# Layer normalisation without affine terms: hand-placed semaphores, tiles of 8 rows and a VectorE loop in place of a scheduled, unrolled kernel

## Chip, cores, metric

One core of a Trainium2 chip. The metric is the device time of one execution in microseconds, the median of several runs; smaller is better. The granted TensorE clock was 1.0 (TensorE does nothing in this kernel). Before: 318.19 us (318.15 to 318.25, 3 runs).

## The reference

```python
x: float32 [32, 512, 1024]            # 16384 rows of 1024; eps = 1e-5
mean = np.mean(x, axis=-1, keepdims=True)
var  = np.var(x, axis=-1, keepdims=True)
out  = (x - mean) / np.sqrt(var + eps)
```

The core has 128 partitions, so 16384 rows are 128 "rows per partition". Below, "a tile of 8 rows" means 8 rows in each of the 128 partitions, 4.2 MB.

## The kernel before

A ring of 50 rows per partition in SBUF holds the tiles. SyncE issues the loads, VectorE (DVE in the profile) takes the statistics of each half row (`bn_stats`), GpSimd (POOL) joins them in nine small steps, ScalarE (ACT) takes the root, VectorE the reciprocal, and ScalarE normalises in place and issues the store. Semaphores are placed by the scheduler. A load must wait until the store that last used its rows has landed.

```python
TILES = (4, 6, 10, 10, 10, 10, 10, 10, 10, 10, 10, 10, 10, 6, 2)
RING = 50
GROUP = 10        # rows normalised together
FINE = 6          # ... in the last LAST tiles
LAST = 3
...
    def rows_of(a, row, K):          # partition p gets K rows that lie together in memory
        return a[row * P : (row + K) * P].rearrange("(p k) d -> p k d", p=P)

    def group(xs, G):
        for k in range(G):
            for s in range(NSUB):    # two halves of 512
                nc.vector.bn_stats(out=stats[:, k, s, :], in_=xs[:, k, s * BN_MAX : (s + 1) * BN_MAX])
        ...                          # nine GpSimd steps, from stats to nmean and ss
        nc.scalar.activation(out=std[:, :G], in_=ss[:, :G], func=AF.Sqrt, bias=eps_t, scale=1.0 / D)
        nc.vector.reciprocal(out=rstd[:, :G], in_=std[:, :G])
        nc.gpsimd.tensor_mul(out=nmr[:, :G], in0=nmean[:, :G], in1=rstd[:, :G])
        for k in range(G):
            nc.scalar.activation(out=xs[:, k, :], in_=xs[:, k, :], func=AF.Identity,
                                 bias=nmr[:, k : k + 1], scale=rstd[:, k : k + 1])
    ...
    with tc.manual_schedule():
        nc.vector.memset(eps_t, eps_val)
        for t, (K, row, pos) in enumerate(plan):
            nc.sync.dma_start(out=ring[:, pos : pos + K, :], in_=rows_of(x2, row, K))
            step = FINE if t >= len(TILES) - LAST else GROUP
            for g in range(0, K, step):
                group(ring[:, pos + g : pos + g + min(step, K - g), :], min(step, K - g))
            nc.scalar.dma_start(out=rows_of(o2, row, K), in_=ring[:, pos : pos + K, :])
```

Of the kernel before, what the change touches and what calls it, by code (L numbers as in the profile page):

```python
# [1 line left out]

# [4 lines left out]


TILES = (4, 6, 10, 10, 10, 10, 10, 10, 10, 10, 10, 10, 10, 6, 2)  # L10

RING = 50


GROUP = 10
FINE = 6
LAST = 3


@with_exitstack  # L20
def kernel(
    ctx: ExitStack,
    tc: tile.TileContext,
    x: bass.AP,
    eps: bass.AP,
    out: bass.AP,
):
    nc = tc.nc
    P = nc.NUM_PARTITIONS
    eps_val = float(eps) if not isinstance(eps, bass.AP) else 1e-5  # L30

    x2 = x.flatten_outer_dims()
    o2 = out.flatten_outer_dims()
    N, D = x2.shape
    BN_MAX = nc.vector.BN_STATS_FMAX
    NSUB = D // BN_MAX
    H = 2 * NSUB
    assert sum(TILES) * P == N

    rings = ctx.enter_context(tc.tile_pool(name="rings", bufs=1))  # L40
    st = ctx.enter_context(tc.tile_pool(name="st", bufs=3))
    sm = ctx.enter_context(tc.tile_pool(name="sm", bufs=10))

    fdt = mybir.dt.float32
    AF = mybir.ActivationFunctionType
    ALU = mybir.AluOpType

    ring = rings.tile([P, RING, D], fdt)
    eps_t = rings.tile([P, 1], fdt)

    def rows_of(a, row, K):
        return a[row * P : (row + K) * P].rearrange("(p k) d -> p k d", p=P)

    def pool_sum(o, terms):
        G = terms.shape[1]
        half = sm.tile([P, GROUP, 2], fdt, name="half")
        nc.gpsimd.tensor_tensor(  # L57
            out=half[:, :G], in0=terms[:, :, 0:2], in1=terms[:, :, 2:4], op=ALU.add
        )
        nc.gpsimd.tensor_tensor(  # L60
            out=o, in0=half[:, :G, 0], in1=half[:, :G, 1], op=ALU.add
        )

    def group(xs, G):
        stats = st.tile([P, GROUP, NSUB, 6], fdt, name="stats")
        for k in range(G):
            for s in range(NSUB):
                nc.vector.bn_stats(  # L68
                    out=stats[:, k, s, :],
                    in_=xs[:, k, s * BN_MAX : (s + 1) * BN_MAX],  # L70
                )

        parts = stats[:, :G].rearrange("p g s (h c) -> p g (s h) c", h=2)
        mean4, m2 = parts[:, :, :, 1], parts[:, :, :, 2]
        nmean = sm.tile([P, GROUP], fdt, name="nmean")
        dev = sm.tile([P, GROUP, H], fdt, name="dev")
        ss = sm.tile([P, GROUP], fdt, name="ss")
        pool_sum(nmean[:, :G], mean4)
        nc.gpsimd.tensor_scalar(  # L79
            out=nmean[:, :G], in0=nmean[:, :G], scalar1=-1.0 / H, scalar2=None, op0=ALU.mult  # L80
        )
        nc.gpsimd.tensor_tensor(  # L82
            out=dev[:, :G],
            in0=mean4,
            in1=nmean[:, :G].unsqueeze(2).to_broadcast([P, G, H]),
            op=ALU.add,
        )
        nc.gpsimd.tensor_mul(out=dev[:, :G], in0=dev[:, :G], in1=dev[:, :G])  # L88
        nc.gpsimd.tensor_scalar(  # L89
            out=dev[:, :G], in0=dev[:, :G], scalar1=float(D // H), scalar2=None, op0=ALU.mult  # L90
        )
        nc.gpsimd.tensor_tensor(out=dev[:, :G], in0=dev[:, :G], in1=m2, op=ALU.add)  # L92
        pool_sum(ss[:, :G], dev[:, :G])
        std = sm.tile([P, GROUP], fdt, name="std")
        nc.scalar.activation(  # L95
            out=std[:, :G], in_=ss[:, :G], func=AF.Sqrt, bias=eps_t, scale=1.0 / D
        )
        rstd = sm.tile([P, GROUP], fdt, name="rstd")
        nc.vector.reciprocal(out=rstd[:, :G], in_=std[:, :G])  # L99
        nmr = sm.tile([P, GROUP], fdt, name="nmr")  # L100
        nc.gpsimd.tensor_mul(out=nmr[:, :G], in0=nmean[:, :G], in1=rstd[:, :G])  # L101
        for k in range(G):
            nc.scalar.activation(  # L103
                out=xs[:, k, :],
                in_=xs[:, k, :],
                func=AF.Identity,
                bias=nmr[:, k : k + 1],
                scale=rstd[:, k : k + 1],
            )

    plan, row, pos = [], 0, 0
    for K in TILES:
        if pos + K > RING:
            pos = 0
        plan.append((K, row, pos))
        row += K
        pos += K

    with tc.manual_schedule():
        nc.vector.memset(eps_t, eps_val)  # L120
        for t, (K, row, pos) in enumerate(plan):
            nc.sync.dma_start(out=ring[:, pos : pos + K, :], in_=rows_of(x2, row, K))
            step = FINE if t >= len(TILES) - LAST else GROUP
            for g in range(0, K, step):
                G = min(step, K - g)
                group(ring[:, pos + g : pos + g + G, :], G)
            nc.scalar.dma_start(out=rows_of(o2, row, K), in_=ring[:, pos : pos + K, :])


# [1 line left out]
_INS = ['x', 'eps']  # L131
_OUTS = [((32, 512, 1024), 'float32')]

_NUMBERS = {'eps': 1e-05}


# [26 lines left out]
```

## Time and profile before

| What | Before |
|---|---|
| time, median | 318.19 us |
| span of the profiled execution | 316.6 us |
| VectorE, ScalarE, GpSimd busy | 49%, 48%, 12% |
| moved by DMA | 134.25 MB, 424 GB/s over the span |
| loads, stores: share of the 16 DMA engines | 49.6%, 49.1% |

Read it from the bottom up: the engines are half idle, and the last two rows say what they wait for. Two of before's lines give the first load and the first store; in this view of instructions in order of time, the columns are start, length, engine, line and operation:

```profile
0.72 8.16 SPq L122 DMA_DIRECT2D ring<-in_x_dram  x6
...
21.58 0.37 ACTq L127 DMA_DIRECT2D out_dram<-ring  x1
```

SyncE issues the first load at 0.72 us and six in a row; ScalarE issues the first store at 21.58 us. Between the two the DMA engines have only loads to do.

### The profile page before, as it was taken

Reading aid. Unit: us, or ns where it says so; the run is one execution under the profiler, and the core shown is the slowest. Engines: PE = TensorE matmul, PEld = TensorE weight load, DVE = VectorE, ACT = ScalarE, POOL = GpSimd, SP = SyncE. Lnnn points to the kernel's source line nnn. Section 1 sums busy time; section 2 is a strip of 40 time slices with the busy share of each in tenths; the row PEclk is TensorE's granted clock in tenths of the full one; section 3 lists DMA queues with packets and bytes.
Section 4 is the critical chain, followed back from the end, with each engine's and each line's share of the span. In section 5 each row is a group of like instructions: output and inputs, shape, how many; then the busy total and the mean of one; then the engine's idle time right before and its main releaser. Section 6 shows DMA issues by size and latency. Waiting matters only on the chain.

```text
span 316.6 us, 712 instructions
## 1 busy us (share of the span) xinstructions
DVE 156.5 (49%) x273; ACT 152.6 (48%) x145; POOL 37.5 (12%) x164
## 2 busy tenths in 40 slices
DVE  0692939539139229229319309409509509654300
ACT  1065329294490391291292192193094094591730
POOL 0202030200300300300300300300300200222200
DMA  8999999999999999999999999999999999999995
GB/s 308 437 424 401 411 466 430 432 419 440 446 435 414 430 457 430 424 419 466 430 424 419 450 435 436 414 430 445 450 414 424 450 438 408 444 421 426 463 407 247
DMA packets 4324, 134.25 MB, mean 424 GB/s; under 512 B 480, under 2 KB 480, under 8 KB 480
## 3 DMA queue, kind: packets, MB, share of 16 engines
q1 hardware_dynamic: 2160, 67.11, 49.6%
q10 hardware_dynamic: 2160, 67.11, 49.1%
q14 instruction: 4, 0.03, 0.0%
HBM read 67.11 MB, written 67.11 MB: 424 GB/s over the span
## 4 chain that ended last, share of the span: by engine, by line
DMA 42%; DVE 26%; another core or an unknown queue 14%; POOL 6%; ACT 5%; issue 3%; SPq 0%; DVEq 0%; POOLq 0%
DMA ring<-in_x_dram 29%; DVE stats L68 26%; DMA out_dram<-ring 13%; ACT ring L103 4%; POOL half L57 1%; POOL dev L89 1%; ACT std L95 1%; POOL dev L92 1%; POOL dev L82 1%; POOL nmean L79 1%; POOL dev L88 1%; POOL nmean L60 1%; POOL ss L60 1%; DVE rstd L99 0%
## 5 line engine op out<-in xcount | busy, mean ns | idle before, releaser
L68 DVE BATCH_NORM_STATS2 stats<-ring 128x6 f32<-128x512 f32 x256 | 153.4, 677 | 92.5 <-DMA ring<-in_x_dram 92.5
L103 ACT ACTIVATE ring<-ring,nmr,rstd 128x1024 f32<-128x1024 f32 x128 | 146.5, 1226 | 8.9 <-POOL nmr L101 8.9
L95 ACT ACTIVATE std<-ss,eps_t 128x10 f32<-128x10 f32 (+3 forms) x16 | 4.8, 301 | 141.7 <-POOL ss L60 141.7
L57 POOL TENSOR_TENSOR half<-stats 128x20 f32<-128x20 f32 (+3 forms) x16 | 3.7, 233 | 243.2 <-DVE stats L68 243.2
L99 DVE RECIPROCAL rstd<-std 128x10 f32<-128x10 f32 (+3 forms) x16 | 3.3, 204 | 51.7 <-ACT std L95 51.7
L89 POOL TENSOR_SCALAR dev<-dev 128x40 f32<-128x40 f32 (+3 forms) x16 | 4.6, 289 | 1.4
L101 POOL TENSOR_TENSOR nmr<-nmean,rstd 128x10 f32<-128x10 f32 (+3 forms) x16 | 3.3, 205 | 10.4 <-DVE rstd L99 10.4
L92 POOL TENSOR_TENSOR dev<-dev,stats 128x40 f32<-128x40 f32 (+3 forms) x16 | 4.1, 259 | 1.3
L79 POOL TENSOR_SCALAR nmean<-nmean 128x10 f32<-128x10 f32 (+3 forms) x16 | 3.9, 244 | 1.4
L82 POOL TENSOR_TENSOR dev<-stats,nmean 128x40 f32<-128x40 f32 (+3 forms) x16 | 3.9, 245 | 1.3
L88 POOL TENSOR_TENSOR dev<-dev 128x40 f32<-128x40 f32 (+3 forms) x16 | 3.8, 239 | 1.3
L57 POOL TENSOR_TENSOR half<-dev 128x20 f32<-128x20 f32 (+3 forms) x16 | 3.4, 212 | 1.3
L60 POOL TENSOR_TENSOR nmean<-half 128x10 f32<-128x10 f32 (+3 forms) x16 | 3.2, 203 | 1.3
L60 POOL TENSOR_TENSOR ss<-half 128x10 f32<-128x10 f32 (+3 forms) x16 | 3.2, 203 | 1.3
L95 ACT ACT_TABLE_LOAD x1 | 1.3, 1283 | 0.9 <-DVE eps_t L120 0.9
L120 DVE MEMSET eps_t<- 128x1 f32 x1 | 0.1, 59 | 0.8 <-PEq L144 0.8
L144 POOL MEMSET const-float32-0.0<- 128x1 f32 x1 | 0.1, 98 | 0.2 <-issue 0.2
L144 POOL MEMSET const-uint8-127<- 128x1 uint8 x1 | 0.1, 102 | 0.0
L144 POOL MEMSET const-bfloat16-1.0<- 128x1 bf16 x1 | 0.1, 101 | 0.0
L144 POOL MEMSET const-float32-1.0<- 128x1 f32 x1 | 0.1, 98 | 0.0
## 6 DMA issues: line engine op xcount, KB each, us to landing
ring<-in_x_dram SPq DMA_DIRECT2D x11, 5120.0 KB, 52.4
out_dram<-ring ACTq DMA_DIRECT2D x11, 5120.0 KB, 41.0
ring<-in_x_dram SPq DMA_DIRECT2D x2, 3072.0 KB, 30.7
out_dram<-ring ACTq DMA_DIRECT2D x2, 3072.0 KB, 22.0
ring<-in_x_dram SPq DMA_DIRECT2D x1, 2048.0 KB, 7.8
out_dram<-ring ACTq DMA_DIRECT2D x1, 2048.0 KB, 22.4
ring<-in_x_dram SPq DMA_DIRECT2D x1, 1024.0 KB, 61.0
out_dram<-ring ACTq DMA_DIRECT2D x1, 1024.0 KB, 11.4
```

Of the source, the lines that this page charges most:

```text
L57: nc.gpsimd.tensor_tensor(out=half[:, :G], in0=terms[:, :, 0:2], in1=terms[:, :, 2:4], op=ALU.add)
L60: nc.gpsimd.tensor_tensor(out=o, in0=half[:, :G, 0], in1=half[:, :G, 1], op=ALU.add)
L68: nc.vector.bn_stats(out=stats[:, k, s, :], in_=xs[:, k, s * BN_MAX : (s + 1) * BN_MAX],)
L79: nc.gpsimd.tensor_scalar(out=nmean[:, :G], in0=nmean[:, :G], scalar1=-1.0 / H, scalar2=None, op0=ALU.mult)
L82: nc.gpsimd.tensor_tensor(out=dev[:, :G], in0=mean4, in1=nmean[:, :G].unsqueeze(2).to_broadcast([P, G, H]), op=ALU.add,)
L88: nc.gpsimd.tensor_mul(out=dev[:, :G], in0=dev[:, :G], in1=dev[:, :G])
L89: nc.gpsimd.tensor_scalar(out=dev[:, :G], in0=dev[:, :G], scalar1=float(D // H), scalar2=None, op0=ALU.mult)
L92: nc.gpsimd.tensor_tensor(out=dev[:, :G], in0=dev[:, :G], in1=m2, op=ALU.add)
L95: nc.scalar.activation(out=std[:, :G], in_=ss[:, :G], func=AF.Sqrt, bias=eps_t, scale=1.0 / D)
L99: nc.vector.reciprocal(out=rstd[:, :G], in_=std[:, :G])
L101: nc.gpsimd.tensor_mul(out=nmr[:, :G], in0=nmean[:, :G], in1=rstd[:, :G])
L103: nc.scalar.activation(out=xs[:, k, :], in_=xs[:, k, :], func=AF.Identity, bias=nmr[:, k : k + 1], scale=rstd[:, k : k + 1],)
```

## The change

The intent: take the scheduler out of the way. One critical section with hand-placed semaphores replaces the scheduled block; all tiles but the last two have 8 rows and go round six fixed places; VectorE runs the middle twelve tiles as a loop of two turns, aligned so that its body sits in one block of instructions; the reciprocals are in that loop; all loads stay on SyncE's queue.

```diff
-TILES = (4, 6, 10, 10, 10, 10, 10, 10, 10, 10, 10, 10, 10, 6, 2)
-RING = 50
+TILES = (8,) * 15 + (6, 2)
+SLOT, SLOTS = 8, 6
+FIRST, TURNS = 3, 2
+BESIDE = ()                       # tiles whose load would go to ScalarE's queue
...
-    with tc.manual_schedule():
...
+    ctx.enter_context(tc.tile_critical(no_gpsimd_drain=True))
...
+    def vector(t, arrived, turn):
+        K, row, at = plan[t]
+        for k in range(K):
+            for s in range(NSUB):
+                i = nc.vector.bn_stats(...)
+                if k == 0 and s == 0:
+                    i._wait_ge(landed[t], arrived)
+        i.then_inc(taken, 1)
+        nc.vector.reciprocal(...)._wait_ge(rooted[t], turn).then_inc(inverse, 1)
...
+    for t in range(FIRST):
+        vector(t, 16, 1)
+    turn = nc.vector.alloc_register("turn")
+    nc.vector.reg_mov(turn, 1)
+    nc.vector.addr_align(128, max_nops=0)
+    with nc.vector.Fori(16, 16 * TURNS + 1, 16) as arrived:
+        for t in range(FIRST, FIRST + SLOTS):
+            vector(t, nc.vector.lower_val(arrived), turn)
+        nc.vector.reg_add(turn, turn, 1)
+    for t in range(FIRST + TURNS * SLOTS, len(plan)):
+        vector(t, 16, 1)
... (GpSimd's and ScalarE's steps: the same instructions, each with a hand-placed wait)
```

More of the change, by code (lines that the diff above doesn't have):

```diff
@@ L7 @@
 from concourse._compat import with_exitstack
-TILES = (4, 6, 10, 10, 10, 10, 10, 10, 10, 10, 10, 10, 10, 6, 2)
-RING = 50
-GROUP = 10
-FINE = 6
-LAST = 3
+TILES = (8,) * 15 + (6, 2)
+SLOT, SLOTS = 8, 6
+FIRST, TURNS = 3, 2
+BESIDE = ()
 @with_exitstack
@@ L38 @@
     assert sum(TILES) * P == N
-    rings = ctx.enter_context(tc.tile_pool(name="rings", bufs=1))
-    st = ctx.enter_context(tc.tile_pool(name="st", bufs=3))
-    sm = ctx.enter_context(tc.tile_pool(name="sm", bufs=10))
     fdt = mybir.dt.float32
@@ L46, with sbuf @@
     ALU = mybir.AluOpType
-    ring = rings.tile([P, RING, D], fdt)
-    eps_t = rings.tile([P, 1], fdt)
+    def sbuf(name, shape):
+        return ctx.enter_context(nc.sbuf_tensor(name, shape, fdt))
+    plan, row = [], 0
+    for K in TILES:
+        plan.append((K, row, row % (SLOT * SLOTS)))
+        row += K
+    ctx.enter_context(tc.tile_critical(no_gpsimd_drain=True))
+    ring = sbuf("ring", [P, SLOT * SLOTS, D])
+    stats = sbuf("stats", [P, SLOT * SLOTS, NSUB, 6])
+    half = sbuf("half", [P, SLOT, 2])
@@ new lines, with places @@
+    dev = sbuf("dev", [P, SLOT, H])
+    ss, nmean, std, rstd, nmr = (
+        sbuf(n, [P, SLOT * SLOTS]) for n in ("ss", "nmean", "std", "rstd", "nmr")
+    )
+    eps_t = sbuf("eps_t", [P, 1])
+    def places(name):
+        out = [nc.alloc_semaphore(f"{name}_{t}") for t in range(FIRST + SLOTS)]
+        for t in range(len(out), len(plan)):
+            looped = t < FIRST + TURNS * SLOTS
+            out.append(out[t - SLOTS] if looped else nc.alloc_semaphore(f"{name}_{t}"))
+        return out
@@ L51, in rows_of, with sixteens @@
+    def sixteens(sems, t):
+        return 16 * sum(1 for s in sems[: t + 1] if s.num == sems[t].num)
+    landed, rooted, stored = places("landed"), places("rooted"), places("stored")
+    taken, inverse, pool, act = map(
+        nc.alloc_semaphore, ("taken", "inverse", "pool", "act")
+    )
     def rows_of(a, row, K):
         return a[row * P : (row + K) * P].rearrange("(p k) d -> p k d", p=P)
-    def pool_sum(o, terms):
-        G = terms.shape[1]
-        half = sm.tile([P, GROUP, 2], fdt, name="half")
-        nc.gpsimd.tensor_tensor(
-            out=half[:, :G], in0=terms[:, :, 0:2], in1=terms[:, :, 2:4], op=ALU.add
-        )
-        nc.gpsimd.tensor_tensor(
-            out=o, in0=half[:, :G, 0], in1=half[:, :G, 1], op=ALU.add
-        )
@@ L64, in group @@
-    def group(xs, G):
-        stats = st.tile([P, GROUP, NSUB, 6], fdt, name="stats")
-        for k in range(G):
-            for s in range(NSUB):
-                nc.vector.bn_stats(
-                    out=stats[:, k, s, :],
-                    in_=xs[:, k, s * BN_MAX : (s + 1) * BN_MAX],
-                )
-        parts = stats[:, :G].rearrange("p g s (h c) -> p g (s h) c", h=2)
-        mean4, m2 = parts[:, :, :, 1], parts[:, :, :, 2]
-        nmean = sm.tile([P, GROUP], fdt, name="nmean")
-        dev = sm.tile([P, GROUP, H], fdt, name="dev")
-        ss = sm.tile([P, GROUP], fdt, name="ss")
-        pool_sum(nmean[:, :G], mean4)
-        nc.gpsimd.tensor_scalar(
-            out=nmean[:, :G], in0=nmean[:, :G], scalar1=-1.0 / H, scalar2=None, op0=ALU.mult
-        )
-        nc.gpsimd.tensor_tensor(
-            out=dev[:, :G],
-            in0=mean4,
-            in1=nmean[:, :G].unsqueeze(2).to_broadcast([P, G, H]),
-            op=ALU.add,
-        )
-        nc.gpsimd.tensor_mul(out=dev[:, :G], in0=dev[:, :G], in1=dev[:, :G])
-        nc.gpsimd.tensor_scalar(
-            out=dev[:, :G], in0=dev[:, :G], scalar1=float(D // H), scalar2=None, op0=ALU.mult
-        )
-        nc.gpsimd.tensor_tensor(out=dev[:, :G], in0=dev[:, :G], in1=m2, op=ALU.add)
-        pool_sum(ss[:, :G], dev[:, :G])
-        std = sm.tile([P, GROUP], fdt, name="std")
-        nc.scalar.activation(
-            out=std[:, :G], in_=ss[:, :G], func=AF.Sqrt, bias=eps_t, scale=1.0 / D
-        )
-        rstd = sm.tile([P, GROUP], fdt, name="rstd")
-        nc.vector.reciprocal(out=rstd[:, :G], in_=std[:, :G])
-        nmr = sm.tile([P, GROUP], fdt, name="nmr")
-        nc.gpsimd.tensor_mul(out=nmr[:, :G], in0=nmean[:, :G], in1=rstd[:, :G])
-        for k in range(G):
-            nc.scalar.activation(
-                out=xs[:, k, :],
-                in_=xs[:, k, :],
@@ new lines, in load @@
+    def load(engine, t):
+        K, row, at = plan[t]
+        return engine.dma_start(
+            out=ring[:, at : at + K, :], in_=rows_of(x2, row, K)
+        ).then_inc(landed[t], 16)
+    owner = {}
+    for t, (K, row, at) in enumerate(plan):
+        gone = sorted({owner[r] for r in range(at, at + K) if r in owner})
+        owner.update((r, t) for r in range(at, at + K))
+        if t in BESIDE:
+            assert not gone
+            load(nc.scalar, t)
+            continue
+        for g in gone[:-1]:
+            nc.sync.wait_ge(stored[g], sixteens(stored, g))
+        dma = load(nc.sync, t)
+        if gone:
+            dma._wait_ge(stored[gone[-1]], sixteens(stored, gone[-1]))
@@ new lines, in vector @@
+    def vector(t, arrived, turn):
+        K, row, at = plan[t]
+        for k in range(K):
+            for s in range(NSUB):
+                i = nc.vector.bn_stats(
+                    out=stats[:, at + k, s, :],
+                    in_=ring[:, at + k, s * BN_MAX : (s + 1) * BN_MAX],
+                )
+                if k == 0 and s == 0:
+                    i._wait_ge(landed[t], arrived)
+        i.then_inc(taken, 1)
+        nc.vector.reciprocal(
+            out=rstd[:, at : at + K], in_=std[:, at : at + K]
+        )._wait_ge(rooted[t], turn).then_inc(inverse, 1)
@@ new lines @@
+    nc.vector.memset(eps_t[:], eps_val)
+    for t in range(FIRST):
[9 more added lines that the diff above has]
+        vector(t, 16, 1)
@@ new lines, with gp @@
+    npool, summed, ready = 0, [], []
+    def gp(i, sem, value):
+        nonlocal npool
+        i._wait_ge(sem, value).then_inc(pool, 1)
+        npool += 1
+        return pool, npool
+    g = nc.gpsimd
+    for t, (K, row, at) in enumerate(plan):
+        parts = stats[:, at : at + K].rearrange("p g s (h c) -> p g (s h) c", h=2)
+        mean4, m2 = parts[:, :, :, 1], parts[:, :, :, 2]
+        nm, d, h = nmean[:, at : at + K], dev[:, :K], half[:, :K]
+        n = gp(
+            g.tensor_tensor(out=h, in0=mean4[:, :, 0:2], in1=mean4[:, :, 2:4], op=ALU.add),
+            taken,
+            t + 1,
+        )
+        n = gp(g.tensor_tensor(out=nm, in0=h[:, :, 0], in1=h[:, :, 1], op=ALU.add), *n)
+        n = gp(
+            g.tensor_scalar(out=nm, in0=nm, scalar1=-1.0 / H, scalar2=None, op0=ALU.mult),
+            *n,
+        )
+        n = gp(
+            g.tensor_tensor(
+                out=d, in0=mean4, in1=nm.unsqueeze(2).to_broadcast([P, K, H]), op=ALU.add
+            ),
+            *n,
+        )
+        n = gp(g.tensor_mul(out=d, in0=d, in1=d), *n)
+        n = gp(
+            g.tensor_scalar(
+                out=d, in0=d, scalar1=float(D // H), scalar2=None, op0=ALU.mult
+            ),
+            *n,
+        )
+        n = gp(g.tensor_tensor(out=d, in0=d, in1=m2, op=ALU.add), *n)
+        n = gp(g.tensor_tensor(out=h, in0=d[:, :, 0:2], in1=d[:, :, 2:4], op=ALU.add), *n)
+        summed.append(
+            gp(
+                g.tensor_tensor(
+                    out=ss[:, at : at + K], in0=h[:, :, 0], in1=h[:, :, 1], op=ALU.add
+                ),
+                *n,
+            )
+        )
+        ready.append(
+            gp(
+                g.tensor_mul(
+                    out=nmr[:, at : at + K], in0=nm, in1=rstd[:, at : at + K]
+                ),
+                inverse,
+                t + 1,
+            )
+        )
@@ L106, in group @@
+    for t, (K, row, at) in enumerate(plan):
+        nc.scalar.activation(
+            out=std[:, at : at + K],
+            in_=ss[:, at : at + K],
+            func=AF.Sqrt,
+            bias=eps_t[:],
+            scale=1.0 / D,
+        )._wait_ge(*summed[t]).then_inc(rooted[t], 1)
+        for k in range(at, at + K):
+            i = nc.scalar.activation(
+                out=ring[:, k, :],
+                in_=ring[:, k, :],
                 func=AF.Identity,
@@ L108, in group @@
                 scale=rstd[:, k : k + 1],
-            )
-    plan, row, pos = [], 0, 0
-    for K in TILES:
-        if pos + K > RING:
-            pos = 0
-        plan.append((K, row, pos))
-        row += K
-        pos += K
-    with tc.manual_schedule():
-        nc.vector.memset(eps_t, eps_val)
-        for t, (K, row, pos) in enumerate(plan):
-            nc.sync.dma_start(out=ring[:, pos : pos + K, :], in_=rows_of(x2, row, K))
-            step = FINE if t >= len(TILES) - LAST else GROUP
-            for g in range(0, K, step):
-                G = min(step, K - g)
-                group(ring[:, pos + g : pos + g + G, :], G)
-            nc.scalar.dma_start(out=rows_of(o2, row, K), in_=ring[:, pos : pos + K, :])
+            ).then_inc(act, 1)
+            if k == at:
+                i._wait_ge(*ready[t])
+        nc.scalar.dma_start(
+            out=rows_of(o2, row, K), in_=ring[:, at : at + K, :]
+        )._wait_ge(act, row + K).then_inc(stored[t], 16)
+    for t in range(len(plan)):
+        if t in owner.values():
+            nc.sync.wait_ge(stored[t], sixteens(stored, t))
 _INS = ['x', 'eps']
```

## The prediction

> **What bounds the kernel now.** I read the page's busy shares first, then the slices and the DMA rows, then the stretches, then the queue waits, and last the beginning and end of the chain.
>
> ```profile
> DVE 156.5 (49%) x273; ACT 152.6 (48%) x145; POOL 37.5 (12%) x164
> ...
> DMA  8999999999999999999999999999999999999995
> ...
> q1 hardware_dynamic: 2160, 67.11, 49.6%
> q10 hardware_dynamic: 2160, 67.11, 49.1%
> ...
> HBM read 67.11 MB, written 67.11 MB: 424 GB/s over the span
> ```
>
> No compute engine is busy half the time, and the DMA digit is 9 in 38 of 40 slices. Loads (q1) and stores (q10) take 49.6% and 49.1% of the sixteen DMA engines: 98.7% of the span is transfers. The 67.11 MB in and 67.11 MB out are what the reference demands once each, so the bytes cannot shrink.
>
> ```profile
> 0.00:8.00 8.00, 0.06 (x1) 1.28 (x1) 0.19 (x4) 1.00 0.82 305
> ...
> 40.00:140.00 100.00, 50.93 (x89) 54.72 (x52) 12.15 (x50) 1.00 1.01 436
> 140.00:240.00 100.00, 51.05 (x88) 50.20 (x48) 9.70 (x40) 1.00 1.00 434
> ...
> 312.00:316.60 4.60, 0.00 (x0) 0.00 (x0) 0.00 (x0) 1.00 0.32 134
> ```
>
> These are stretches: window and length, busy DVE, ACT and POOL with counts, TensorE clock, DMA share, GB/s. The rate is flat at 434 to 436 GB/s through the middle and falls only in the first 8 us (305) and in the last 4.6 us (134). 134.2 MB at 434 GB/s is 309.3 us; the span is 316.6. So 7.3 us at most lie outside the transfer floor, 2.3% of the span, and part of them no kernel escapes.
>
> ```profile
> SPq L122 <- DMA out_dram<-ring: 222.2, 9, 35.1
> ...
> DVE stats L68 <- DMA ring<-in_x_dram: 92.5, 14, 8.8
> ```
>
> SyncE waits 222 us for stores to free ring rows and VectorE 92.5 us for loads. Both waits are back pressure of the full DMA engines, not causes. The chain of waits puts 26% on the statistics line; with the DMA share at 1.00 in the same stretches, I choose not to read that as a bound.
>
> From the packet records of the trace I take four things. Data moves from 2.08 us to 315.58 us of the span, 313.5 us. A packet is one partition's contiguous rows: 309 ns for 8 KB, 611 for 16 KB, 912 for 24 KB, 1514 for 40 KB, that is about 8 ns plus 301 ns per 8 KB. The first packets run long (all engines together lose 0.9 us each), and when the first store begins at 22 us another 0.75 us is lost. Fifteen engines end between 313.4 and 314.5 us; one alone ends at 315.58. That one stood aside for an 8 KB instruction fetch at 54.3 and at 195.5 us, each a 302 ns gap with a neighbouring packet 540 to 630 ns too long: about 0.9 us each, 1.8 us together, which is just its lateness.
>
> **What the Trainium skill says.** "DMA: Bandwidth & Descriptors", section "Where 436 GB/s comes from", gives 435.2 GB/s as the ceiling of the sixteen SBUF ports. The trace agrees with 434 to 436; the 358 GB/s it names for one core's share of HBM does not bind here. The same page, "Issuing engines are not separate DMA queues", says that DMAs of all issuers end on the same sixteen engines: so which queue issues the loads is worth only issue time, 0.33 us of SyncE per load here (and all loads are on SyncE already). "Runtime: NRT & Kernel Launch", section "Instruction fetch mechanics", says that instructions are streamed by DMA in blocks, and that a taken branch whose target lies outside the two-block window must fetch it. The trace agrees that fetches go by DMA (8,192-byte records, smaller than the page's 16 KiB blocks); no branch is in it yet.
>
> **The change, part by part.**
>
> 1. Tiles. Before: 15 tiles, mostly of 10 rows. After: 15 of 8, one of 6, one of 2. Each engine moves 8 partitions per tile and direction, so its packets rise from 2x15x8 = 240 to 2x17x8 = 272: 32 more at 8 ns, 0.26 us, and four more 9 ns semaphore packets, 0.04 us. **+0.3 us**, all on the path because DMA is the bound. An estimate: a 32 KB packet by the same line is 8 + 4x301 = 1212 ns.
>
> 2. First tile of 8 rows instead of 4. Before, statistics began at 8.56 us. Four more rows are 2.1 MB, 4.84 us at 434 GB/s: 13.4 us. Eight rows take 16 x 0.598 = 9.6 us of statistics (from 11.97 for 20), to 23.0; statistics to first normalisation took 3.5 us in the first tile of before, a little more for more rows, so ACT starts near 26.7 and ends 8 x 1.15 = 9.2 us later: first store at 36 us instead of 21.6. Is there load work until then? Six places are 48 rows, 25.2 MB, issued without any wait; at 36 us some 14.3 MB have come. Yes. Store 0 then shares the engines, needs 4.2 MB at half of 434, 19.3 us, and ends near 56 us, when 4.2 MB more have come: 18.5 of 25.2. Load 6 is released with 6.7 MB still queued. **0 us.**
>
> 3. Steady state. One tile moves 8.4 MB, 19.3 us. VectorE needs 9.6 us and then stands about 3.4 us for the sums and the root before its reciprocal: 13.0 us. ACT needs 9.2 + 0.3 us. Both fit under 19.3. A place is in compute for about 9.6 + 3.8 + 9.2 = 22.6 us, of a round of 6 x 19.3 = 116 us; the other 93 us it sits in a DMA queue. Neither queue empties both ways at once. **0 us.**
>
> 4. End. The 6- and 2-row loads both wait only for the store of tile 9. By the half-rate schedule above, stores end at 56 + 19.3 t, tile 9 near 230; loads run on without a gap and the last lands near 279 us, leaving about 28 rows (15 MB, 34 us) to store. The last two tiles need some 17 us from there. Before had 20 us of stores after its last landing at 295.9 and 12 us of work. Slack in both. **0 us.**
>
> 5. Loop and fewer VectorE instructions. 273 become 3x17 + 102 + 18 = 171 in the program (the 102 run twice). The aligned loop is meant to sit in one fetched block, so I expect at most one of the two fetches that made one engine late. Without either, the end falls to the next engine, 314.5: 1.1 us. I take most of it: **-0.8 us**.
>
> 6. Critical section. Its own end (SyncE's six or so last waits, a drain, a meeting of engines) comes before the one of the kernel, which took 0.7 us (315.8 to 316.5). I estimate half to one of that, and perhaps 0.1 at the start: **+0.5 us**.
>
> Hand-placed semaphores, reciprocals and the chain of GpSimd sums: same instructions, in the shade of the transfers. Sum: 318.19 + 0.3 - 0.8 + 0.5 = **318.2 us**.
>
> **The rivals.**
>
> - *The pitch of HBM rows.* Partitions now start 32 KB apart, a power of two, where most were 40 KB apart. The same DMA page, "Latency and other measured facts", reports 207 GB/s at a 512 KiB pitch against 214 padded, and half at 4 MiB, for large powers of two. For it: the streams run in lock step. Against: 32 KB is far below those, and the before kernel's 4-row and 2-row stores, at pitches of 16 and 8 KB, kept 611 and 309 ns per packet, on the common line. A 3% loss of rate would make 328 us; I give it 3%.
> - *A queue runs dry.* If hand-ordered VectorE work (reciprocal before the next statistics) held back stores, both queues could empty at the start or end. For it: five fewer microseconds of fine splitting at the end, a later first store. Against: the 15 us of slack above. It would make 320 to 324.
> - *The loop refetches.* If each turn fetches blocks again, several fetches at 0.9 us fall on the same DMA engine and make it the straggler: +1 to +3 us, 319 to 321. VectorE's own stalls would be hidden.
> - *The ends shrink.* If no engine is late and the section costs nothing, 316.5 us, still only 0.5% less.
>
> **Range and chances.** The sum's terms are each under 1 us; the unknown ones (section end, fetches, straggler) may all go one way, and the lop-sided risks are upward. Predicted 318.2 us, range 316.8 to 320.0. Faster by 2% needs 311.8 us, below the 309.3 us of pure transfer plus the 2 us start and 1 us end, so 1%; slower by 2% needs 324.6, by pitch or starvation, 3%; within 2%, 96%.
>
> **What would show it.** Right: DMA digits of 9 from the second slice to the next to last; 434 GB/s in the middle; 2448 packets on each of q1 and q10; first store near 36 us; VectorE's waits still on loads; an end of transfers between 313.5 and 315 us and a tail after it of over 1 us. Wrong: a middle below 430 GB/s (pitch), a slice with a digit under 9 (dry queue), more than four mid-run instruction packets on the same engine (refetch), or loads issued late at the start.

## The result

The changed kernel took **317.97 us** (317.67 to 318.23, 4 runs) beside 318.17 us (317.93 to 318.25, 4 runs) for the kernel before: ratio 0.9994, 95% interval 0.9977 to 1.0012. A ratio here is the mean time of one kernel's runs over that of the other's in the same rounds, so it is not quite the ratio of the quoted medians. When the changed kernel was run again beside three experiments, it took 317.98 us (ratio 0.9990, 0.9976 to 1.0003).

The page of the changed kernel, in the order of the lines shown of before (busy shares; slices; DMA queues, q1 for SyncE's loads, q10 for ScalarE's stores, q14 for instructions):

```profile
DVE 156.8 (50%) x274; ACT 153.0 (48%) x146; POOL 39.3 (12%) x174
...
DMA  8999999999999999999999999999999999999995
...
q1 hardware_dynamic: 2448, 67.11, 49.6%
q10 hardware_dynamic: 2448, 67.11, 49.1%
q14 instruction: 3, 0.02, 0.0%
HBM read 67.11 MB, written 67.11 MB: 424 GB/s over the span
```

The same busy times, the same row of nines, the same 424 GB/s. What differs is the number of packets, 2448 a queue instead of 2160, and three instruction packets after the first microseconds instead of four. The stretches of the changed kernel (window and length; DVE, ACT, POOL busy with counts; TensorE clock; DMA share; GB/s):

```profile
0.00:8.00 8.00, 0.06 (x1) 1.28 (x1) 0.19 (x4) 1.00 0.82 328
...
40.00:140.00 100.00, 57.64 (x101) 58.88 (x57) 13.93 (x60) 1.00 1.00 430
140.00:240.00 100.00, 48.97 (x85) 50.23 (x49) 11.60 (x50) 1.00 1.01 434
...
312.00:316.60 4.60, 0.00 (x0) 0.00 (x0) 0.00 (x0) 1.00 0.38 162
```

The DMA share of the middle is 1.00 as before; its rate from 40 to 140 us is 430 GB/s where before had 436, and the kernel with the new tiles alone has 430 there too. The last stretch has a DMA share of 0.38 where before had 0.32: the engines end closer together. Queue waits and VectorE's wait, then the issues in order of time:

```profile
SPq L87 <- DMA out_dram<-ring: 228.2, 10, 56.8
...
DVE stats L111 <- DMA ring<-in_x_dram: 81.6, 14, 12.0
```

```profile
0.93 2.92 SPq L87 DMA_DIRECT2D ring<-in_x_dram  x6
...
35.64 0.37 ACTq L211 DMA_DIRECT2D out_dram<-ring  x1
```

SyncE and VectorE wait on the same things as before, SyncE 6 us longer and VectorE 11 us less. The first load is issued 0.21 us later, the first store 14 us later, and the second of these costs nothing visible.

**Where the time went.** A finer table than the page can be had from the packet records of the trace. Each of the 16 DMA engines closes the last store with a 4-byte packet, so each engine's end is known. "Mean engine" is the mean of the 16 ends less the mean of the 16 first starts; "last engine late by" is the latest end less the mean end; "fetches" are the 8 KB instruction packets from 3 us on, as long as data moves. (A packet record names no DMA engine; where one engine is over 2.5 us late, its packet for the store before last comes after other engines' last one and has to be left out.)

| kernel | first packet, us | mean engine, us | last engine late by, us | fetches | last packet to end of span, us |
|---|---|---|---|---|---|
| before | 1.75 | 311.7 | 1.7 | 4 | 1.30 |
| after | 1.93 | 311.6 | 0.9 | 3 | 1.78 |
| after, run again | 1.93 | 311.7 | 0.6 | 3 | 1.78 |

The mean engine works 311.6 to 311.7 us before and after the change. What the change moved is at the ends: the first packet 0.18 us later, 0.48 us more between the last packet and the end of the span, and the last engine 0.7 to 1.1 us less late. These nearly cancel.

All of this is inside the span, from the first instruction to the last. In the rounds that both kernels shared the mean span is 316.3 us for both; the time outside it is 1.95 us in before (1.95 to 2.00 in all rounds that list it) and 1.63 to 1.64 us in the changed kernel. So inside the span the effects cancel completely, and the 0.2 to 0.3 us by which the changed kernel is shorter lie outside it, where no trace looks; their cause is not known.

(The prediction counted its packet times from a wrong zero: its 2.08, 315.58, 54.3 and 195.5 us are 1.75, 315.25, 54.0 and 195.1 us of the span. Its lengths are not touched by that.)

### The profile page after: what moved, and what is told of

Same layout as the page of the kernel before. It is cut to its first block, busy times and chain, and to the rows that moved or that the text cites. A ratio compares the mean times of both kernels' runs of the same rounds, so it can differ in the third digit from the quotient of the medians.

```text
span 316.6 us, 693 instructions
## 1 busy us (share of the span) xinstructions
DVE 156.8 (50%) x274; ACT 153.0 (48%) x146; POOL 39.3 (12%) x174
## 3 DMA queue, kind: packets, MB, share of 16 engines
q1 hardware_dynamic: 2448, 67.11, 49.6%
q10 hardware_dynamic: 2448, 67.11, 49.1%
## 4 chain that ended last, share of the span: by engine, by line
DMA 54%; another core or an unknown queue 18%; ACT 9%; DVE 9%; POOL 2%; issue 1%; SPq 0%; ACTq 0%
DMA ring<-in_x_dram 31%; DMA out_dram<-ring 24%; ACT ring L202 9%; DVE stats L111 8%; ACT std L194 0%; SPq L87 0%; POOL dev L167 0%; POOL nmr L184 0%; DVE rstd L118 0%; POOL dev L172 0%; POOL nmean L156 0%; POOL dev L160 0%; POOL dev L165 0%; POOL half L150 0%
## 5 line engine op out<-in xcount | busy, mean ns | idle before, releaser
L111 DVE BATCH_NORM_STATS2 stats<-ring 128x6 f32<-128x512 f32 x256 | 153.5, 678 | 82.2 <-DMA ring<-in_x_dram 81.6
L194 ACT ACTIVATE std<-ss,eps_t 128x8 f32<-128x8 f32 (+2 forms) x17 | 5.1, 300 | 134.7 <-POOL ss L176 134.3
L150 POOL TENSOR_TENSOR half<-stats 128x16 f32<-128x16 f32 (+2 forms) x17 | 3.9, 231 | 233.0 <-DVE stats L111 233.0
L118 DVE RECIPROCAL rstd<-std 128x8 f32<-128x8 f32 (+2 forms) x17 | 3.4, 200 | 55.4 <-ACT std L194 55.4
L167 POOL TENSOR_SCALAR dev<-dev 128x32 f32<-128x32 f32 (+2 forms) x17 | 5.0, 293 | 1.5
L184 POOL TENSOR_TENSOR nmr<-nmean,rstd 128x8 f32<-128x8 f32 (+2 forms) x17 | 3.5, 203 | 11.9 <-DVE rstd L118 11.9
L172 POOL TENSOR_TENSOR dev<-dev,stats 128x32 f32<-128x32 f32 (+2 forms) x17 | 4.3, 254 | 1.4
L160 POOL TENSOR_TENSOR dev<-stats,nmean 128x32 f32<-128x32 f32 (+2 forms) x17 | 4.1, 239 | 1.4
L165 POOL TENSOR_TENSOR dev<-dev 128x32 f32<-128x32 f32 (+2 forms) x17 | 4.0, 235 | 1.3
L156 POOL TENSOR_SCALAR nmean<-nmean 128x8 f32<-128x8 f32 (+2 forms) x17 | 4.0, 232 | 1.5
L173 POOL TENSOR_TENSOR half<-dev 128x16 f32<-128x16 f32 (+2 forms) x17 | 3.6, 213 | 1.3
```

The costliest lines, as they stand in the source:

```text
L111: i = nc.vector.bn_stats(out=stats[:, at + k, s, :], in_=ring[:, at + k, s * BN_MAX : (s + 1) * BN_MAX],)
L118: nc.vector.reciprocal(out=rstd[:, at : at + K], in_=std[:, at : at + K])._wait_ge(rooted[t], turn).then_inc(inverse, 1)
L150: g.tensor_tensor(out=h, in0=mean4[:, :, 0:2], in1=mean4[:, :, 2:4], op=ALU.add),
L156: g.tensor_scalar(out=nm, in0=nm, scalar1=-1.0 / H, scalar2=None, op0=ALU.mult),
L160: g.tensor_tensor(out=d, in0=mean4, in1=nm.unsqueeze(2).to_broadcast([P, K, H]), op=ALU.add),
L165: n = gp(g.tensor_mul(out=d, in0=d, in1=d), *n)
```

## The experiments

Twelve runs follow: eleven other kernels, and the changed kernel once more. The theory: the transfers bind everywhere, and each part of the change is worth under 1 us, at the start, at the end, or in the lateness of one DMA engine through instruction fetches. The rival: two large effects cancel.

### Tiles alone

```diff
 (the kernel before)
-TILES = (4, 6, 10, 10, 10, 10, 10, 10, 10, 10, 10, 10, 10, 6, 2)
-RING = 50
-GROUP = 10
-FINE = 6
+TILES = (8,) * 15 + (6, 2)
+RING = 48
+GROUP = 8
+FINE = 8
```

> The kernel before with the tile sizes of the change alone (15 of 8 rows, then 6 and 2, in 48 rows of ring), its own scheduling otherwise kept. Theory (transfers are the bound, every part of the change moves under 1 us): 2448 packets a queue, first store near 36 us instead of 21.6, and a time within 0.7 us of before, by the packets 0.3 us longer. Rival (two large effects cancel in the change: small tiles cost over 1% and hand-placed semaphores win it back): over 1% longer than before, 321 us or more.

Measured: 318.51 us beside 318.26, ratio 1.0011 (0.9997 to 1.0025). The tile sizes alone cost 0.25 us, which cannot be told from zero. No large loss is hidden in them for the semaphores to win back, and the rival falls.

### No computing at all

```diff
 (the changed kernel, without VectorE's and GpSimd's work and ScalarE's activations)
-        )._wait_ge(act, row + K).then_inc(stored[t], 16)
+        )._wait_ge(landed[t], sixteens(landed, t)).then_inc(stored[t], 16)
```

> The changed kernel without any computing: each store waits only for its own load, so the output is the input, wrong on purpose. Same loads, stores, places, critical section. Theory (the bound is transfers): 316 to 318 us, at most 2 us under the changed kernel. Rival (a compute chain or its waits sets part of the time): clearly shorter, under 313 us.

Measured: 317.73 us (317.15 to 317.81), ratio 0.9980 to before (0.9966 to 0.9994). Its output is wrong, which doesn't matter for the time. The page of this kernel:

```profile
POOL 0.2 (0%) x4
...
DMA  8999999999999999999999999999999999999996
```

An execution in which no engine computes is 0.24 us shorter than the changed kernel (which ran in other rounds; against before in their own rounds the ratios are 0.9980 and 0.9990 to 0.9994). All of the normalisation, its semaphores, its order and its engines are worth that much together. This is the strongest single piece of evidence: with these tiles and queues, the best that any rearrangement of the computing could have won is about 0.1%.

### VectorE with all statistics twice

```diff
+                nc.vector.bn_stats(out=spare[:, at + k, s, :],
+                                   in_=ring[:, at + k, s * BN_MAX : (s + 1) * BN_MAX])
```

> The changed kernel with all statistics taken twice: VectorE needs 19.2 + 3.4 = 22.6 us per 8-row tile, over the 19.3 us of the transfers, and becomes the bound. Theory: 13 us to the first landing + 512 x 0.598 = 306 us of statistics + 17 x 3.4 = 58 us of standing before the reciprocals + about 9 us for the last rows: 386 us, with DMA digits falling under 9. If the transfers still bound: 318 us.

Measured: 379.75 us (2 runs), ratio 1.193. The expected value was 386. The page:

```profile
DVE 307.2 (81%) x530; ACT 153.1 (41%) x146; POOL 39.3 (10%) x174
...
DMA  8999999999989999899899979989998255190947
```

Here the digits of DMA fall below 9, in the last part to 1 and 0, and VectorE's waits for loads come to 12.0 us, all of it the first landing. This is what the profile looks like when VectorE is the bound, and it is not what the profile of before or after looks like. The estimate was 6 us long; the largest term that was off is VectorE's standing before its reciprocals, 45.2 us and not 58.

### The loop written out

```diff
-    turn = nc.vector.alloc_register("turn")
-    nc.vector.reg_mov(turn, 1)
-    nc.vector.addr_align(128, max_nops=0)
-    with nc.vector.Fori(16, 16 * TURNS + 1, 16) as arrived:
-        for t in range(FIRST, FIRST + SLOTS):
-            vector(t, nc.vector.lower_val(arrived), turn)
-        nc.vector.reg_add(turn, turn, 1)
+    for t in range(FIRST, FIRST + TURNS * SLOTS):
+        n = sixteens(landed, t)
+        vector(t, n, n // 16)
```

> The changed kernel with VectorE's loop written out (no branch, no alignment, 290 instead of 171 instructions in its program). Theory (an instruction fetch costs one DMA engine about 0.9 us and only the last engine counts): two VectorE fetches fall on one DMA engine in the run, that engine ends last, and the time is 0 to 1.1 us longer than the changed kernel, about 318.8 us. Rival (fetches don't matter to the end, the last engine is chance): equal within 0.2 us with the last engine not the one that fetched.

Measured: 318.59 us (318.49 to 318.74), ratio 1.0012 (0.9998 to 1.0025). The changed kernel was not in those rounds. (The page counts 274 VectorE instructions; the 290 of the expectation are in no view.) The kernel with the tiles alone was in them, and differs from this one by the critical section and the hand-placed semaphores: the mean span is 316.4 us there and 316.8 us here, the time outside it 2.10 and 1.76 us, so the section costs about 0.4 us inside the span and 0.1 us of time in all. A second kernel then served as a repeat beside it. It was meant to add 544 empty instructions:

```diff
 (in vector(), after the reciprocal)
+        for _ in range(32):
+            nc.vector.nop(nofuse=True)
```

> The unrolled kernel with 32 empty instructions on VectorE after every reciprocal, 544 in all: [...]four more instruction fetches of 8 KB, and 1 to 2 us more per tile on an engine with 6 us to spare. Theory (VectorE's fetches all fall on one DMA engine, about 0.9 us each, and the last engine sets the end): about 3.6 us over unrolled, 322 us, with one DMA engine ending some 4 us after the others. If each fetch falls on another engine: at most 1 us over. If fetches cost the transfers nothing: equal to unrolled (318.6).

> The changed kernel once more, so that it stands in the same rounds as the three below. Expected 317.6 to 318.3 us, as its four runs.

The build dropped the empty instructions, so this kernel has the same VectorE instructions as the unrolled one, and its expectation was not tested. As a repeat it is useful: 318.42 us, against 317.98 us for the changed kernel in the same rounds. Five runs each, and the two do not overlap (318.37 to 318.79, 317.83 to 318.05). The loop is worth about 0.4 us; the prediction had 0.8.

### Four more fetches

Memsets are not dropped, so the same question was put again:

```diff
 (in vector() of the unrolled kernel, after the reciprocal)
+        for n in range(32):
+            nc.vector.memset(spare[:, 32 * t + n : 32 * t + n + 1], 0.0)
```

> In place of the empty instructions, which were dropped from the program: the unrolled kernel with 32 one-element memsets on VectorE after every reciprocal, 544 in all, [...]four more VectorE fetches of 8 KB; about 2 us more per tile on an engine with 6 us to spare. Theory (VectorE's fetches all fall on one DMA engine, about 0.9 us each, and the last engine sets the end): about 3.6 us over unrolled, near 322 us, one DMA engine ending some 4 to 5 us after the middle one. If each fetch falls on another engine: at most 1 us over. If fetches cost the transfers nothing: equal to unrolled (318.4 to 318.6).

Measured: 323.37 us (321.98 to 325.06, 6 runs), ratio 1.0168 (1.0137 to 1.0199). The memsets take 59 ns each but overlap: the 32 of a tile are done in 0.48 us, a quarter of what was expected, and VectorE's wait for loads hardly changes: 80.1 us, after 81.6 in the changed kernel. So VectorE is not late, and yet the execution is 4.8 us longer than the unrolled kernel's 318.59. The six runs lie in two groups, three of 321.98 to 322.37 us and three of 324.37 to 325.06 us. The profile is of a run of the first group (322.37 us, 3.7 us over the profiled run of the unrolled kernel); what the second group adds was not traced. Its instruction packets, and its end in stretches of 2 us:

```profile
q14 instruction: 8, 0.07, 0.0%
```

```profile
312.00:314.00 2.00, 0.00 (x0) 0.00 (x0) 0.00 (x0) 1.00 0.79 332
314.00:316.00 2.00, 0.00 (x0) 0.00 (x0) 0.00 (x0) 1.00 0.08 33
316.00:318.00 2.00, 0.00 (x0) 0.00 (x0) 0.00 (x0) 1.00 0.06 25
318.00:320.50 2.50, 0.00 (x0) 0.00 (x0) 0.00 (x0) 1.00 0.02 7
```

Eight fetches instead of four, just the four that were expected. Then look at the DMA share from 314 us on: 0.06 to 0.08, and one engine of sixteen is 0.0625. Fifteen engines are done by 314.8 us, and one goes on alone until 318.8 us at 25 to 33 GB/s, where a sixteenth of 434 GB/s is 27. In the packet records the last engine is 4.8 us behind the mean against 1.4 in the unrolled kernel, 3.4 us for four fetches: 0.85 each. That it is one and the same engine each time can be read from the 4-byte packets that close each load, one from every engine. The latest of them is 1.9 us behind the median of its load before the fetch at 72.1 us, and 3.1, 3.9, 4.6, 5.6 and 6.3 us behind after the fetches at 72.1, 112.1, 165.0, 213.0 and 263.5 us, while the next latest stays at 1.4 to 1.6. This is the mechanism in plain sight: a fetch takes its time out of one DMA engine, the fetches that the added VectorE code brings fall on the same one, and a DMA is only complete when its last engine is.

### Without the alignment

```diff
-    nc.vector.addr_align(128, max_nops=0)
```

> The changed kernel without the alignment of VectorE's loop. If the loop then lies across more blocks than are held and is fetched again at its turn, one or two more VectorE fetches appear and the time is 0 to 1 us longer. If the blocks are still held, equal to the changed kernel within 0.2 us and three mid-run fetches as before; then the alignment is worth nothing here.

Measured: 318.13 us (317.90 to 318.43), against 317.98 in the same rounds, and three fetches, at 56.8, 81.4 and 94.8 us where the changed kernel has 55.7, 80.9 and 94.2. The loop gives its gain; the alignment gives none that shows here.

### A second critical section

```diff
+    with tc.tile_critical(no_gpsimd_drain=True):
+        with nc.sbuf_tensor("spare", [P, 1], fdt) as spare:
+            nc.vector.memset(spare[:], 0.0)
     ctx.enter_context(tc.tile_critical(no_gpsimd_drain=True))
```

> The changed kernel after a second, tiny critical section that holds one memset. By the theory a section costs what the profile shows of it, about 0.4 us before the first load and 0.2 to 0.4 at its end; this one lies wholly before the first load, so the first packets start 0.5 to 1.0 us later and the time grows as much. If the section's cost were hidden: no change.

Measured: 318.67 us (318.53 to 318.79), 0.69 us over the changed kernel in the same rounds. The first loads of this kernel, in order of time:

```profile
1.63 2.94 SPq L90 DMA_DIRECT2D ring<-in_x_dram  x6
```

1.63 us instead of 0.93: 0.70 us, and the time grew by 0.69. What delays the first load is paid in full. The change's own section delays it by 0.21 us and adds 0.48 us after the last packet.

### One load on the other queue

```diff
-BESIDE = ()
+BESIDE = (1,)
```

> The changed kernel with its second load issued on ScalarE's queue instead of SyncE's. By the theory, which queue issues a load is worth nothing once the DMA engines are full: within 0.3 us of the changed kernel. For the loss of 0.75 us when the first store begins: if it is the first use of ScalarE's queue, it moves to the start, where packets run long anyway, and loads near 38 to 42 us keep 1213 ns (about 0.5 us less time); if it is the first writing to memory, it stays where it was.

Measured: 317.89 us (317.80 to 318.08), ratio 0.9989 (0.9975 to 1.0003), level with the changed kernel. ScalarE's queue now moves data from 3.6 us on, but the stretch of long load packets stays with the first store. It costs 1.1 us per engine here, 0.76 in the changed kernel. In each kernel it begins 1 to 2 us after ScalarE issues the first store, wherever that falls:

| kernel | first store issued, us | long load packets begin, us |
|---|---|---|
| no computing | 13.18 | 14.75 |
| before | 21.58 | 23.65 |
| after | 35.64 | 37.67 |
| one load on the other queue | 45.19 | 46.23 |

So they are not the price of the queue's first use. They come with the first store, before its own first packet starts (39.67 us in the changed kernel); what stretches them was not found.

### VectorE busier, within its slack

```diff
+                if k % 2 == 0:
+                    nc.vector.bn_stats(out=spare[:, at + k, s, :],
+                                       in_=ring[:, at + k, s * BN_MAX : (s + 1) * BN_MAX])
```

> The changed kernel with every second row's statistics taken twice, the second time into a spare tile: 8 more of them per tile, 4.8 us, so VectorE needs 14.4 + 3.4 = 17.8 us of the 19.3 us that a tile's transfers take. Theory (VectorE lies in the shade of the transfers): same time, 318 to 319 us, and its waits for loads shrink from 82 us to under 15. Rival (the statistics on the chain of waits are part of the bound): 318 + 17 x 4.8 = up to 400 us.

Measured: 320.74 us (320.19 to 321.98), ratio 1.0086 (1.0067 to 1.0104). The rival's 400 us is far away, and the transfers still bind, but the expected 318 to 319 was missed. VectorE's waits did shrink:

```profile
DVE 231.2 (73%) x402; ACT 153.1 (48%) x146; POOL 39.3 (12%) x174
```

```profile
DVE stats L112 <- DMA ring<-in_x_dram: 12.2, 1, 12.2
```

VectorE waits only for the first tile, and 74 us more of its work (231.2 less 156.8) cost 2.5 us against before. Two explanations were open: more instructions to fetch (five fetches instead of three, last engine late by 3.0 us), or less slack. The last run was chosen to part them:

```diff
 (the changed kernel, in vector(), before i.then_inc(taken, 1))
+        i = nc.vector.tensor_reduce(out=spare[:, at : at + 1], in_=ring[:, at : at + K // 2, :],
+                                    op=ALU.max, axis=mybir.AxisListType.XY)
```

> dve_half_more put 4.8 us more on VectorE per tile, in 8 more instructions, and took 2.8 us longer than the changed kernel where the same time was expected. Here one long instruction per tile (a maximum over four of its rows, into a spare column, before the sums) puts some 4 us more on VectorE with one more instruction per tile. If the 2.8 us came from more instructions to fetch (the loop of 150 no longer fits its block): within 0.5 us of the changed kernel, 317.8 to 318.5 us, three or four mid-run fetches, although VectorE is as busy. If they came from VectorE being busy (less slack, later stores): again 320 us or more.

Measured: 322.51 us (321.35 to 323.74), ratio 1.0133 (1.0113 to 1.0153). The expectation that named fetches is refuted for this kernel: it has four, and it is longer still. The other one, 320 us or more, came true. But the two kernels do not lose their time in the same place. Two stretches of this one, to be held against the 430 and 434 GB/s of the changed kernel:

```profile
40.00:90.00 50.00, 39.73 (x51) 26.06 (x27) 7.02 (x30) 1.00 1.01 422
90.00:140.00 50.00, 40.29 (x52) 26.76 (x27) 7.02 (x30) 1.00 1.00 425
```

The DMA engines are never idle (share 1.00), but load packets run long. In the packet records this happens each time one store ends and the next begins, some 20 us apart. The kernels side by side:

| kernel | mean engine, us | long packets after 55 us, us per engine | last engine late by, us | fetches | time, us |
|---|---|---|---|---|---|
| no computing | 311.6 | 0.0 | 0.7 | 0 | 317.73 |
| after | 311.6 | 0.3 | 0.9 | 3 | 317.97 |
| tiles alone | 311.7 | 0.1 | 1.4 | 5 | 318.51 |
| unrolled | 311.7 | 0.1 | 1.4 | 4 | 318.59 |
| memsets | 311.8 | 0.3 | 4.8 | 8 | 323.37 |
| half the statistics twice | 312.0 | 0.5 | 3.0 | 5 | 320.74 |
| one long instruction a tile | 314.3 | 2.7 | 2.5 | 4 | 322.51 |

With half the statistics twice, the mean engine is only 0.4 us slower and the loss is a late engine, as with fetches: by the packets that close each load it falls back by 0.7, 0.9 and 0.9 us at the fetches at 38.1, 71.1 and 142.7 us. But two more engines end 2.1 and 2.5 us after the median one, and fell back in small steps without a fetch. With one long instruction a tile, all engines are slower. So for the first the fetches are a likely cause of most of the loss, read from the trace and not tested alone; for the second the cause is open. It is not the bound of VectorE as in the doubled kernel, where DMA digits fall, and it is not a fetch. Nor is it that stores are issued with less of a queue before them: without computing, the second to the fourteenth store are issued 6.6 us before the first engine is done with the store ahead, and no packet runs long after 55 us; here the second store is issued 5.6 us before that, and the others 7 us and more. Whether it is the long instruction itself these runs cannot tell.

No version here beats the changed kernel by more than the spread of the runs. The one with a load on the other queue is level with it, and the one without any computing bounds what is to be had.

## Why the prediction was right

Predicted 318.2 us, measured 317.97 and 317.98. By its own steps:

1. **Transfers bind.** Shown: without any computing the time is 317.73 us, and the mean engine takes 311.6 to 311.7 us before, after and without computing.
2. **Tiles, +0.3 us.** The count was right (2448 packets a queue), and so was the length: 1213 ns for a 32 KB packet, estimated 1212. The tiles alone took 0.25 us more time, which cannot be told from zero. In the changed kernel the 0.3 us does not show in the mean engine, which is the same to 0.1 us. The long packets at the start and at the first store cost 0.3 us less than before (1.6 against 1.9 us per engine, taken over all long packets of the run) and hide it. These losses were seen in the prediction but taken as fixed.
3. **First tile of 8 rows, 0 us.** First store predicted at 36 us, issued at 35.64. Its lateness is free.
4. **Steady state, 0 us.** Right. Doubling VectorE's statistics did make it the bound, at 379.75 us. The step took all work under 19.3 us as free, and there it was too simple: the two kernels with VectorE at 17 to 18 us a tile lost 2.5 and 4.1 us against before. The change does not go there.
5. **End, 0 us.** Right in substance, off in the middle: the last load landed at 288 us in the packet records, not 279. The last store was issued at 298.0 us, and the one before it ended at 312.4 us, so it had 14 us of slack where the prediction had 15 (its own 34 less 17 are 17). Its 12 us of work at the end of before are 8.3 us: the last load landed at 295.9 us and the last store was issued at 304.2 us.
6. **Loop, -0.8 us.** Mechanism right, shown by the memsets; the size was half. The unrolled kernel is 0.4 us longer in the same rounds. In the profiled execution the last engine is 0.7 to 1.1 us less late than before. The prediction had found the late engine by following packets without gaps from one to the next, which cannot always tell two engines apart; the lone engine at the end of the memset kernel is the proof that it lacked. The packets that close each store bear it out for before: the latest engine falls from 1.9 to 2.5 us behind the median at the fetch at 54.0 us, and from 2.5 to 3.4 at that at 195.1 us. Not all lateness is of fetches: without computing no fetch falls into the run, and the last engine is still 0.7 us late, about as late as in the changed kernel.
7. **Critical section, +0.5 us.** Right: 0.2 us before the first load (0.1 had been said) and 0.5 us after the last packet (half to one of 0.7 had been said), 0.7 in all against 0.5. The end of the kernels with a section, from the last packet on, takes 1.55 to 1.79 us, that of the two without 1.27 and 1.30. By the kernels with the tiles alone and with the loop written out, the section and the semaphores cost 0.4 us inside the span.

Of the rivals, the pitch of 32 KB does no harm (1213 ns per packet, 434 GB/s from 140 to 240 us). The 430 GB/s from 40 to 140 us stand right at the sign of harm that the prediction named (below 430), but the kernel without computing has the same pitch and 434 GB/s there. No queue ran dry: no digit below 9 between the first and the last slice. The loop does not refetch at its turn: three fetches in the run. The rival of shrinking ends was the nearest, and half of it came true: the last engine is less late, but the section is not free.

That the sum lands within 0.3 us owes something to luck: the packets' +0.3 was eaten by smaller losses elsewhere, the loop's gain and the section's cost each came out some tenths from where they were put, and the prediction had no term for the time outside the span, where the whole difference to before lies.

## What to carry to other kernels

When loads and stores fill the DMA engines, first run the kernel with the computing taken out: if that time is the same, no order of the computing and no semaphore will be worth a per cent with those transfers, and what is left inside the span is what comes before the first load, what follows the last store, and the one DMA engine that finishes last. Code size can count even on an engine with half its time idle, because its instructions come over one of the DMA engines that carry the data; a loop in place of unrolled code won 0.4 us here, and 544 needless small instructions cost 4.8 us. Slack is not entirely free either: two kernels that used up most of VectorE's idle time lost about 1% without becoming bound by it.

## What the Trainium skill lacked or had wrong

- "Runtime: NRT & Kernel Launch", section "Instruction fetch mechanics": it calls the cost of crossing a block mostly hidden, and blocks 16 KiB. Here fetches are 8,192-byte packets, and in a kernel bound by transfers each VectorE fetch made one and the same DMA engine about 0.8 to 0.9 us late; 544 more VectorE instructions, with four more fetches, cost 4.8 us. The section does not say that one engine's fetches fall on one DMA engine, nor what they cost the data there.
- The same section warns of taken branches. A loop of two turns, aligned or not, showed no additional fetch (three in both) and was 0.4 us faster than unrolled code; the aligned and unaligned times were 317.98 and 318.13 us.
- "DMA: Bandwidth & Descriptors", section "Where 436 GB/s comes from": its 435.2 GB/s is reached, 434 to 436 in the middle with loads and stores mixed. Its statement that for transfers between HBM and SBUF the HBM limit of about 358 GB/s binds does not hold here, with one core running; the page itself allows this under its measured bandwidths, where about 358 GB/s is for both cores of a pair streaming.
- The same page, "Latency and other measured facts": it gives no figure for a pitch as small as 32 KB. A pitch of 32 KB costs nothing (1213 ns per 32 KB packet, on one line with the other sizes).
- No page has: the loss when the first store begins beside running loads, 0.75 us per DMA engine and more, which stays at the first store when the queue was used before; and the cost of a critical section, 0.2 us before the first load and 0.5 us after the last packet, 0.69 us for a second one ahead of it.
